# A feed-forward stage that hands products to GpSimd and multiplies by tokens that already carry their norm

## The chip, the cores and the metric

The kernel runs on one core of a Trainium2 chip. The metric is the device time of one execution in microseconds, and shorter is better. Five engines work side by side, each through its own queue, in order: TensorE multiplies matrices (PE in the profile, PEld is its weight load), VectorE does arithmetic on tensors (DVE), ScalarE does activations, casts and copies (ACT), GpSimd does elementwise work on SBUF alone (POOL), and SyncE issues DMAs (SP). An instruction that waits for another engine holds up everything behind it in its own queue.

## The reference

Two layers act on `x`, 512 tokens by 1024 features. Each has a token mixer (differential attention in layer 0, gated linear attention in layer 1) beside a cross-attention into 256 memory tokens, one output projection, and a gated feed-forward stage. The change lies in the feed-forward stage:

```
def conv_ffn(h, w_up, conv_w, conv_b, w_down):
    u = h @ w_up                                   # 1024 -> 2 * 2816
    c = depthwise_causal_conv(u, conv_w) + conv_b  # width 3 over the tokens
    a, g = jnp.split(c, 2, axis=-1)
    return (jax.nn.silu(g) * a) @ w_down           # 2816 -> 1024
...
        h = rms_norm(x, ffn_norm[i])
        x = x + conv_ffn(h, w_up[i], conv_w[i], conv_b[i], w_down[i])
```

`rms_norm` multiplies each token by one number of its own, 1/rms, and each feature by a gain. The number of a token can be applied to `h` ahead of the product or to `u` behind it.

## The kernel before

Features lie on the partitions and the 512 tokens along a row. `x` is eight tiles `xT[k]` of 128 x 512. All products are in fp32r with both operands split in two, a rounded part (`hi`, a cast on ScalarE) and the rest (`lo`, a subtraction on VectorE), and each product takes three matmuls: hi by hi, hi by lo, lo by hi.

Weights come in blocks of 128 x 1024 (`raw`, three buffers, loaded in the order of a plan) and are split into `whi` and `wlo` (six buffers each, `WB`): a cast on ScalarE (L255) and a subtraction on VectorE (L258). A block can be split only when the matmuls that read the buffer's last content are done.

The feed-forward stage, `ffn`, goes through three parts of 4, 4 and 3 up tiles (`HALVES`). An up tile `q` has two column groups `n`, and for each PE runs two products of 24 matmuls: `ua` for the linear half and `ug` for the gated half. The eight tokens' tiles `tokens[k]` are taken one after the other within a product, three matmuls each. They hold `x` times the gain, without 1/rms. That number comes later: `row_scales` computes it for all tokens as the tile `rB` behind the first `ua` and `ug`, and `conv` multiplies each product, in PSUM, by `rB` on VectorE (L1165). Then ScalarE takes the last tap and the bias (L1167), VectorE adds the two other taps (L1168, L1169), ScalarE takes the Silu of the gated half (L1333), and VectorE multiplies the halves (L1334). The result is split (`parts_of`, L1190 on ScalarE and L1191 on VectorE) into `mid` tiles. In most parts four sums and differences of each two such tiles are made too, by `combine`, on GpSimd except for a part's last up tile (L1198 to L1201), since the product with `w_down` uses a scheme of seven products for eight (`seven`); the sums of weight blocks for it are made on GpSimd by `combined` (L287 to L290).

The order of PE's instructions is that of the code. On the other engines a scheduler sets it when the program is built. PSUM has eight banks in four groups of two (`mm`, `sm`, `lg`, `tp`); the up products take them in turn, and the down products by a rule of their own.

Of the kernel before, what the change touches and what calls it, by code (L numbers as in the profile page):

```python
# [11 lines left out]
F32 = mybir.dt.float32  # L12
# [9 lines left out]
S = 512  # L22
# [63 lines left out]
def _pieces():  # L86

    plan = []

    def piece(key, name, i, ks, *ranges):  # L90
        plan.append((key, name, i, ks, ranges))

    for l in range(2):
        if l == 0:
            w = "w_in_diff"
            piece(("qk", 0), w, 0, K8, (0, 256), (768, 1024))
            for key in ORDER:
                if key[0] == "qk":
                    p = key[1]
                    piece(key, w, 0, K8, (256 * p, 256 * p + 256), (768 + 256 * p, 1024 + 256 * p))  # L100
                elif key[0] == "kv":
                    piece(key, "w_mem_kv", key[1], K8, (0, 512))
                elif key[0] == "vm":
                    p = key[1]
                    piece(key, w, 0, K8, (1536 + 256 * p, 1792 + 256 * p), (2304, 2560))
                else:
                    p = key[1]
                    piece(key, w, 0, K8, (1536 + 256 * p, 2048 + 256 * p))
        else:
            w = "w_in_gla"  # L110
            piece(("gm", 1), w, 0, K8, (2304, 2576))
            for c in range(5):
                piece(("g", c), w, 0, K8, (512 * c, min(512 * c + 512, 2304)))
        for i, part in enumerate(PASS[l]):
            for c, ks in part:
                piece(("o", l, i, c), "w_out", l, ks, (256 * c, 256 * c + 256))
        base = 0
        for nq in HALVES:
            for q in range(base, base + nq):
                piece(("ua", l, q), "w_up", l, K8, (256 * q, 256 * q + 256))  # L120
# [18 lines left out]

TURNS = ('mm', 'mm', 'sm', 'sm', 'lg', 'lg', 'tp', 'tp')  # L140
# [42 lines left out]
def trunk(ctx, tc, head_d, x_t, mem_t, wpack, cols_a_d, cols_d, conv_d, gate_d, rel_bias, diff_lambda, consts, onehot, out):  # L183
# [94 lines left out]
    def combined(raw, n):  # L278
# [4 lines left out]
        r, wsum = full(raw), sum_pool[0].tile([128, WTILE], F32, name="wsum", bufs=2)  # L283
        a12, a22, a11, a21 = (r[:, :, i] for i in range(4))
        sv = wsum[:, :512 * pairs].rearrange("p (i j c) -> p i j c", i=4, j=pairs)
        s1, s2, s3, s4 = (sv[:, i] for i in range(4))
        ADD.tensor_add(s1, a21, a22)  # L287
        ADD.tensor_sub(s3, a11, a21)
        ADD.tensor_sub(s2, s1, a11)
        ADD.tensor_sub(s4, a12, s2)  # L290
        A.copy(full(h0)[:, :, :3], r[:, :, :3])
        V.tensor_sub(full(l0)[:, :, :3], r[:, :, :3], full(h0)[:, :, :3].bitcast(F32))
        m = slice(0, 512 * pairs)
        A.copy(h1[:, m], wsum[:, m])
        V.tensor_sub(l1[:, m], wsum[:, m], h1[:, m].bitcast(F32))
        out = []
        for j in range(pairs):
            own = lambda t, i: t[:, 512 * j + 128 * i:512 * j + 128 * i + 128]
            new = lambda t, i: t[:, 128 * (pairs * i + j):128 * (pairs * i + j) + 128]
# [3 lines left out]
        return out  # L303

    def make_block(raws=None):
# [9 lines left out]
        if plan[i][0][0] == "dn":  # L315
            made[i] += combined(raw, n)
# [8 lines left out]
    ADD = G  # L325


    def weights(key, by_block=False):
# [3 lines left out]
        if i + 1 < len(plan) and plan[i + 1][0][0] in ("dn", "dw"):  # L332
            limit = first_of[i + 1] + 1
# [814 lines left out]
    def ffn(pool, l, acc):  # L1148
        rB = pool.tile([128, S], F32, name="rB", bufs=1)
        sum_pool[0] = pool  # L1150
        old = list(zip(xh, xl))
        nu = [0]
# [4 lines left out]
        def up(parts, n, ops):  # L1157
            i = nu[0]
            nu[0] += 1
            p = bank(TURNS[i % 8])  # L1160
            product(p, parts, n, ops)
            return p

        def conv(p, j):
            V.tensor_mul(p, p, rB)  # L1165
# [27 lines left out]
        left, right = blk(0, 256), blk(1, 256)  # L1193

        def combine(b2, b1, bh, bl, fh, fl, E):
            t = pool.tile([128, 2 * S], F32, name="tsum", bufs=1)
# [5 lines left out]
            h, lo = (pool.tile([128, 2 * S], F32R, name="mid2", bufs=9) for _ in range(2))  # L1202
            for c in ((blk(0, S), blk(1, S)) if E is V else (blk(0, 2 * S),)):
                parts_of(t[:, c], h[:, c], lo[:, c])
            two = lambda hi, lw, c: (hi[:, c], lw[:, c])
            return [(fh, fl), two(bh, bl, left), two(bh, bl, right), two(h, lo, q[3]),
                    two(h, lo, q[0]), two(h, lo, q[1]), two(h, lo, q[2])]
# [4 lines left out]
        def down(base, nq, mids, pairs, tags, last, acc2):  # L1212
            first = used[0]
            whole = [plan[first + c][0][0] == "dw" for c in range(4)]
            sizes = [1 if plan[i][0][0] != "dn" else 2 for i, _, _ in order]
            live = sum(sizes[first_of[first]:done[0]])
            banks, seen = {}, [set() for _ in range(4)]

            def refill():
                nonlocal live  # L1220
                while done[0] < min(len(order), first_of[min(used[0] + 2, len(plan))]) and live + sizes[done[0]] <= WB:
                    live += sizes[done[0]]
                    make_block()

            def start(c):
                assert plan[used[0]][0][1:] == (l, base, c)
                used[0] += 1
                if whole[c] and l == 0:
                    banks[c] = [bank("lg"), bank("tp")]
                else:  # L1230
                    ta, tb = (("mm", "sm"), ("lg", "tp"))[(c + tags) % 2]
                    banks[c] = [bank(t) for t in ((ta, tb) if whole[c] else (ta, ta, tb, tb))]
                refill()

            def release(c, m):
                nonlocal live
                piece = first + c
                if m == nq - 1 or m % 2:
                    live -= 1 if whole[c] else 2
                    refill()  # L1240

            def seven(c, m, some=steps):
                for i in some:
# [7 lines left out]
                release(c, m)  # L1251
                if m == nq - 1:
                    made[first + c] = None
# [17 lines left out]
            def eight(c, n, m0, m1, total=nq):  # L1271
                parts = made[first + c]
                product(banks[c][n], parts, n, pairs, range(2 * m0, 2 * m1), 2 * total)

            if all(whole):
                refill()
                for c0 in (0, 2):
                    cs = (c0, c0 + 1)
                    for c in cs:
# [3 lines left out]
                        release(c, 1)  # L1283
                    for c in cs:
# [4 lines left out]
                        release(c, nq - 1)  # L1289
                        made[first + c] = None  # L1290
                return
            refill()
# [8 lines left out]
            if whole[3]:  # L1301
                start(3)
                while done[0] < first_of[first + 4]:
                    make_block()
# [5 lines left out]
                for t, tag, queue in ((left, "mm", nc.sync), (right, "sm", nc.scalar)):  # L1310
                    p = bank(tag)[:, :S // 2]
# [5 lines left out]
        base, tokens, acc2 = 0, old, None  # L1317
        for part, nq in enumerate(HALVES):
            mids, pairs = [], []
            nu[0] = 0  # L1320
            last = part == len(HALVES) - 1
            for q in range(base, base + nq):
                wa = weights(("ua", l, q))
                wg, c2, ops = None, [], []
                for n in range(2):
                    ua = up(wa, n, tokens)
                    wg = wg or weights(("ug", l, q))
                    ug = up(wg, n, tokens)
# [4 lines left out]
                    A.activation(cg, cg, AF.Silu)  # L1333
                    V.tensor_mul(ca, ca, cg)  # L1334
                    c2.append(ca)
                    if n == 0 or last:
                        ops += [mid_tile(), mid_tile()]
                        parts_of(ca, *ops[-2:])
                        pairs.append(ops[-2:])
                    else:  # L1340
                        m = mid_tile()
                        ops += [m[:, left], m[:, right]]
                        parts_of(ca[:, left], *ops[-2:])
                if last:
                    ops[2:] = [t[:, left] for t in ops[2:]]
                if not last or l == 1:
                    mids.append(combine(*c2, *ops, V if q == base + nq - 1 else ADD))
# [7 lines left out]
            down(base, nq, mids, pairs, nu[0] // 4 % 2, last, acc2)  # L1355
# [88 lines left out]
```

## Time and profile before

| | us |
|---|---|
| median of 3 runs | 1149.63 (1149.50 to 1149.68) |
| profiled execution, its own time | 1150.36 |
| its span, first to last instruction | 1148.5 |
| PE busy | 1142.7 (99%) |
| VectorE busy | 871.2 (76%) |
| ScalarE busy | 592.0 (52%) |
| GpSimd busy | 193.2 (17%) |

The profiled execution took 0.73 us more than the median, and 1.86 us of its time lies outside its span. Layer 0's feed-forward stage begins on PE at 240.69 us and its third up tile at 284.67 us; in layer 1 these are 792.43 and 836.40 us. Durations in the rows are of single instructions, and neighbours on an engine overlap by up to 0.1 us. A matmul of 128 x 512 has a modelled end: its length in a row is 0.39 us, but the next one starts 0.22 to 0.23 us after it.

### The profile page before, as it was taken

To read this page: it belongs to the slowest core of one execution; us is meant where nothing else is said; L and a number is where in the kernel's file an instruction comes from. 1 tells how busy PE (TensorE), PEld (TensorE's weight loads), DVE (VectorE), ACT (ScalarE), POOL (GpSimd) and SP (SyncE) were. 2 spreads that over 40 slices of the span, in tenths; PEclk is the share of its full clock that TensorE was granted. 3 is DMA by queue.
4 is the path that set the end of the run, shared out by engine and by line. 5 is a ranking of instruction groups with operands and counts; after the bars stand their busy time and mean duration, and the time that the engine had idled before them with its cause. 6 is when DMAs were issued, how large, how long until landed. Compare 5 with 4: busy or idle time off the path is not lost.

```text
span 1148.5 us, 16655 instructions
## 1 busy us (share of the span) xinstructions
PE 1142.7 (99%) x6311; PEld 985.1 (86%) x6311; DVE 871.2 (76%) x1455; ACT 592.0 (52%) x1032; POOL 193.2 (17%) x230
## 2 busy tenths in 40 slices
PE   9999999999999999999999999999999999999998
PEld 7888888888899888988888888988888988899887
DVE  8576778688789677977677637777887977797777
ACT  6676686555454354434457634535644444453442
POOL 0000000001543125500000000000135403360340
PEclk9999999999999999999999999999999999999999
DMA  9522242133214322343252220333241342234212
GB/s 293 173 83 84 78 142 74 58 109 110 92 57 146 111 77 80 96 144 100 69 182 70 100 94 12 101 125 119 74 126 40 127 149 74 61 91 143 92 46 102
DMA packets 39662, 117.83 MB, mean 103 GB/s; under 512 B 4767, under 2 KB 7256, under 8 KB 39582
## 3 DMA queue, kind: packets, MB, share of 16 engines
q1 hardware_dynamic: 39150, 116.37, 31.8%
q8 instruction: 50, 0.82, 0.3%
q10 hardware_dynamic: 432, 0.39, 0.1%
q14 instruction: 30, 0.25, 0.1%
HBM read 112.54 MB, written 4.21 MB: 102 GB/s over the span
## 4 chain that ended last, share of the span: by engine, by line
PE 99%; DMA 0%; DVE 0%; ACT 0%; issue 0%
PE ps_mm L365 6%; PE ps_mm L367 6%; PE ps_mm L366 6%; PE ps_mm L387 6%; PE ps_mm L388 6%; PE ps_mm L389 6%; PE ps_lg L1247 5%; PE ps_sm L388 5%; PE ps_sm L389 5%; PE ps_sm L387 5%; PE ps_mm L1247 4%; PE ps_tp L388 4%; PE ps_lg L388 4%; PE ps_tp L387 4%; PE ps_lg L387 4%; PE ps_tp L389 4%
## 5 line engine op out<-in xcount | busy, mean ns | idle before, releaser
L258 DVE TENSOR_TENSOR wlo<-raw,whi 128x1024 fp32r<-128x1024 f32 (+4 forms) x174 | 194.2, 1127 | 77.0 <-ACT whi L255 76.4
L255 ACT CAST whi<-raw 128x1024 fp32r<-128x1024 f32 (+4 forms) x174 | 168.0, 976 | 124.2 <-PE ps_sm L388 29.8
L365 PE MATMUL ps_mm<-whi,xsh 128*128 128x512 f32 (+2 forms) x328 | 126.2, 385 | 0.0
L367 PE MATMUL ps_mm<-whi,xsl 128*128 128x512 f32 (+2 forms) x328 | 123.0, 375 | 0.0
L366 PE MATMUL ps_mm<-wlo,xsh 128*128 128x512 f32 (+2 forms) x328 | 122.8, 374 | 0.0
L387 PE MATMUL ps_mm<-xsh,whi 128*128 128x512 f32 x278 | 109.3, 393 | 0.0
L388 PE MATMUL ps_mm<-xsl,whi 128*128 128x512 f32 x278 | 108.4, 390 | 0.0
L389 PE MATMUL ps_mm<-xsh,wlo 128*128 128x512 f32 x278 | 108.2, 389 | 0.0
L387 PE MATMUL ps_sm<-xsh,whi 128*128 128x512 f32 x218 | 84.8, 389 | 0.0
L388 PE MATMUL ps_sm<-xsl,whi 128*128 128x512 f32 x218 | 84.8, 389 | 0.0
L389 PE MATMUL ps_sm<-xsh,wlo 128*128 128x512 f32 x218 | 84.8, 389 | 0.0
L365 PEld LDWEIGHTS ps_mm<-whi,xsh 128*128 128x128 f32 x328 | 61.7, 188 | 11.4 <-issue 1.0
L367 PEld LDWEIGHTS ps_mm<-whi,xsl 128*128 128x128 f32 x328 | 61.7, 188 | 11.3
L366 PEld LDWEIGHTS ps_mm<-wlo,xsh 128*128 128x128 f32 x328 | 61.8, 188 | 10.1
L387 PE MATMUL ps_lg<-xsh,whi 128*128 128x512 f32 x160 | 62.2, 389 | 0.0
L388 PE MATMUL ps_lg<-xsl,whi 128*128 128x512 f32 x160 | 62.2, 389 | 0.0
L389 PE MATMUL ps_lg<-xsh,wlo 128*128 128x512 f32 x160 | 62.2, 389 | 0.0
L387 PE MATMUL ps_tp<-xsh,whi 128*128 128x512 f32 x160 | 62.2, 389 | 0.0
L388 PE MATMUL ps_tp<-xsl,whi 128*128 128x512 f32 x160 | 62.2, 389 | 0.0
L389 PE MATMUL ps_tp<-xsh,wlo 128*128 128x512 f32 x160 | 62.2, 389 | 0.0
L389 PEld LDWEIGHTS ps_mm<-xsh,wlo 128*128 128x128 f32 x278 | 52.2, 188 | 11.0
L387 PEld LDWEIGHTS ps_mm<-xsh,whi 128*128 128x128 f32 x278 | 52.2, 188 | 10.8 <-issue 0.3
(382 smaller groups left out, 2835.4 us busy)
## 6 DMA issues: line engine op xcount, KB each, us to landing
raw<-in_wpack_dram SPq DMA_DIRECT2D x178, 512.0 KB, 3.5
xt<-in_x_t_dram SPq DMA_DIRECT2D x15, 256.0 KB, 5.2
raw<-in_wpack_dram SPq DMA_DIRECT2D x15, 256.0 KB, 3.1
raw<-in_wpack_dram SPq DMA_DIRECT2D x8, 384.0 KB, 3.0
xres<-xt SPq DMA_DIRECT2D x8, 256.0 KB, 3.2
xt<-xres SPq DMA_DIRECT2D x8, 256.0 KB, 5.8
out_dram<-xt SPq DMA_DIRECT2D x7, 256.0 KB, 2.0
bt<-bias_d SPq DMA_DIRECT2D x6, 256.0 KB, 4.1
```

Of the source, the lines that this page charges most:

```text
L255: ins = A.copy(hi[:, c], raw[:, c])
L258: V.tensor_sub(lo[:, c], raw[:, c], hi[:, c].bitcast(F32))
L365: mm(p, sh[k][:, blk(b)], hi, start=k == 0, stop=False)
L366: mm(p, sh[k][:, blk(b)], lo, start=False, stop=False)
L367: mm(p, sl[k][:, blk(b)], hi, start=False, stop=k == KT - 1)
L387: mm(p, hi[:, blk(n)], bh, start=i == first, stop=False)
L388: mm(p, hi[:, blk(n)], bl, start=False, stop=False)
L389: mm(p, lo[:, blk(n)], bh, start=False, stop=i == last)
L1247: mm(banks[c][b][:, h], w, v, start=b not in seen[c], stop=m == nq - 1 and t == 2 and i in close)
```

## The change

From the third up tile of each layer on (`SCALED = 2`) the products use scaled tokens, `fresh`. While the first two up tiles run, each `xT[k]` is multiplied by `rB` on GpSimd (`scaled`), by the gain on ScalarE, and split by `parts_of`: eight products, sixteen ScalarE instructions and eight VectorE subtractions a layer. Three tokens are made behind each of the second and third column groups and two behind the fourth. Up tiles 2 to 10 then need no product with `rB` in `conv`. The gating product is made on GpSimd except in the last up tile of each part. The sums of `combine` and `combined` share two buffers (`wsum`; before, there were two and one), `mid2` has eight buffers for nine, PSUM banks are taken in one rotation by all products, and weight blocks are asked for whenever two (or one) of the six buffers have been used up (`refill`, `release`), in the up products too. `dynamic_dma_scratch_size=512` frees memory for the tokens' tiles `hsc`. `SEVEN` is empty, so that the code for it (`up_by_seven`, `token_sums`, `plain`) makes no instruction. PE has as many instructions as before, of the same shapes.

```
+SCALED = 2
+SEVEN = ()
...
-        def conv(p, j):
-            V.tensor_mul(p, p, rB)
+        def conv(p, j, scaled):
+            if not scaled:
+                V.tensor_mul(p, p, rB)
...
+        def scaled(k):
+            t = ctile()
+            G.tensor_mul(t, xT[k], rB)
+            A.activation(t, t, AF.Copy, scale=c_ffn(l, k))
+            return t
+
+        def scaled_token(k):
+            t = scaled(k)
+            if k < 6:
+                y = pool.tile([128, 2 * S], F32R, name="hsc", bufs=6)
+                hi, lo = y[:, :S], y[:, S:]
+            else:
+                hi, lo = split_tiles()
+            parts_of(t, hi, lo)
+            return hi, lo
...
             for q in range(base, base + nq):
-                wa = weights(("ua", l, q))
+                if q == SCALED:
+                    tokens = fresh
...
-                    ca = conv(ua, 2 * q + n)
-                    cg = conv(ug, 22 + 2 * q + n)
+                    cn = ca[n] if ca else conv(ua, 2 * q + n, q >= SCALED)
+                    cg = conv(ug, 22 + 2 * q + n, q >= SCALED)
                     A.activation(cg, cg, AF.Silu)
-                    V.tensor_mul(ca, ca, cg)
+                    end = q == base + nq - 1
+                    (V if end else G).tensor_mul(cn, cn, cg)
...
+                    if 0 < 2 * q + n < 4:
+                        fresh += [scaled_token(k) for k in range(len(fresh), min(len(fresh) + 3, KT))]
...
+        def take(n):
+            nb[0] += n
+            return [bank(TURNS[i % 8]) for i in range(nb[0] - n, nb[0])]
+
+        def refill():
+            nonlocal live
+            while done[0] < min(len(order), first_of[min(used[0] + 2, len(plan))]) and live + sizes[done[0]] <= WB:
+                live += sizes[done[0]]
+                make_block()
...
+        def up(i, n):
+            p, = take(1)
+            product(p, whole_piece(i), n, tokens)
+            if n == 1:
+                release(i, 2, True)
             return p
```

GpSimd's queue in layer 0, before, from the first sums of up tiles on (`cvo` are results of `conv`, `raw` is a weight block):

```order
L1198 TENSOR_TENSOR tsum_2833<-cvo_2819 128x256
L1200 TENSOR_TENSOR tsum_2833<-cvo_2753,cvo_2819 128x256
L1199 TENSOR_TENSOR tsum_2833<-cvo_2753,tsum_2833 128x256
L1201 TENSOR_TENSOR tsum_2833<-cvo_2753,tsum_2833 128x256
L1198 TENSOR_TENSOR tsum_2997<-cvo_2983 128x256
L1200 TENSOR_TENSOR tsum_2997<-cvo_2917,cvo_2983 128x256
L1199 TENSOR_TENSOR tsum_2997<-cvo_2917,tsum_2997 128x256
L287 TENSOR_TENSOR wsum_3211<-raw_3053 128x256
```

The same queue in the changed kernel, from the fourth token (`xt_1744`) to the sums of the second up tile:

```order
L1294 TENSOR_TENSOR cvo_2950<-xt_1744,rB_2659 128x512
L1294 TENSOR_TENSOR cvo_2956<-xt_1746,rB_2659 128x512
L1294 TENSOR_TENSOR cvo_2962<-xt_1748,rB_2659 128x512
L1428 TENSOR_TENSOR cvo_2935<-cvo_2935,cvo_2940 128x512
L1294 TENSOR_TENSOR cvo_3045<-xt_1750,rB_2659 128x512
L1294 TENSOR_TENSOR cvo_3052<-xt_1752,rB_2659 128x512
L1428 TENSOR_TENSOR cvo_3031<-cvo_3031,cvo_3036 128x512
L1271 TENSOR_TENSOR wsum_3061<-cvo_3031 128x256
```

Eight token products and four gating products of 128 x 512 have come in among the sums; those of the last two tokens stand behind the gating product of the second up tile's first column group (`cvo_2935`).

ScalarE's queue in layer 0, before, from the last weight casts ahead of the end of the second up tile on (its last product is `ps_tp_2957`):

```order
L255 CAST whi_3043<-raw_2889 128x1024 [waits DMAHW1_49,PE_49]
L255 CAST whi_3049<-raw_3010 128x1024 [waits DMAHW2_49,PE_49]
L1167 ACTIVATE cvo_2988<-ps_tp_2957,cv0_81 128x512 [waits DVE_49]
L1333 ACTIVATE cvo_2988<-cvo_2988 128x512 [waits DVE_49,Activation_49]
L1190 CAST mid_2994<-cvo_2983 128x256 [waits DVE_49]
L1190 CAST mid2_3002<-tsum_2997 128x1024 [waits Pool_49]
L1167 ACTIVATE cvo_3081<-ps_mm_3018,cv0_81 128x512 [waits DVE_49]
```

The same place in the changed kernel (that last product is `ps_tp_3005`, `cvo_3045` is the seventh token, `cvo_3052` the eighth):

```order
L1242 ACTIVATE cvo_3036<-ps_tp_3005,cv0_81 128x512 [waits DVE_49]
L1295 ACTIVATE cvo_3045<-cvo_3045,cols_80 128x512 [waits Pool_49]
L1295 ACTIVATE cvo_3052<-cvo_3052,cols_80 128x512 [waits Pool_49]
L258 CAST whi_3074<-raw_2997 128x1024 [waits DMAHW2_49,PE_49]
L1426 ACTIVATE cvo_3036<-cvo_3036 128x512 [waits DVE_49,Activation_49]
L1265 CAST mid_3042<-cvo_3031 128x256 [waits Pool_49]
L1265 CAST xsh_3048<-cvo_3045 128x512 [waits Activation_49]
L1265 CAST xsh_3055<-cvo_3052 128x512 [waits Activation_49]
```

The casts of the last two tokens' `hi` parts now stand behind the Silu of the second up tile's last product and behind a cast that waits for GpSimd's gating of it.

PE's queue at the third up tile of layer 0, in the changed kernel, from the sixth token on (the weights are `whi_2878` and `wlo_2879`):

```order
L398 MATMUL ps_mm_3080<-hsc_2965,whi_2878 128x512 [waits Activation_49]
L399 MATMUL ps_mm_3080<-hsc_2965,whi_2878 128x512 [waits DVE_49]
L400 MATMUL ps_mm_3080<-hsc_2965,wlo_2879 128x512
L398 MATMUL ps_mm_3080<-xsh_3048,whi_2878 128x512 [waits Activation_49]
L399 MATMUL ps_mm_3080<-xsl_3049,whi_2878 128x512 [waits DVE_49]
L400 MATMUL ps_mm_3080<-xsh_3048,wlo_2879 128x512
```

Where the kernel before reads tokens that were ready before the stage began, each token's first two matmuls now wait for a cast and for a subtraction.

More of the change, by code (lines that the diff above doesn't have):

```diff
@@ L303, in combined, with by_seven, sum_tile @@
         return out
+    def by_seven(i):
+        key = plan[i][0]
+        return key[0] == "dn" or key[0] == "ua" and key[2] in SEVEN
+    def sum_tile():
+        return sum_pool[0].tile([128, WTILE], F32, name="wsum", bufs=2)
     def make_block(raws=None):
@@ L314, in make_block @@
             made.append([])
-        if plan[i][0][0] == "dn":
-            made[i] += combined(raw, n)
+        if by_seven(i):
+            made[i] += combined(raw, n, int(plan[i][0][0] == "ua" and not made[i]))
         else:
@@ new lines, in up_by_seven @@
+        def up_by_seven(i):
+            b, seen = take(4), set()
+            where = [(2, left), (0, left), (0, right), (1, left), (3, right), (2, right), (3, left)]
+            for m, ks in enumerate(((6, 7), (4, 5), (0, 1), (2, 3))):
+                while len(made) <= i or len(made[i]) <= m:
+                    refill()
+                part = made[i][m]
+                if m == 0:
+                    for n in range(2):
+                        product(b[n], part, n, [tokens[k] for k in ks], range(2), 99)
+                else:
+                    for r in steps:
+                        c, h = where[r]
+                        (hi, lo), (vh, vl) = part[r], sums_of[ks][r]
+                        for t, (w, v) in enumerate(((hi, vh), (hi, vl), (lo, vh))):
+                            mm(b[c][:, h], w, v, start=c > 1 and c not in seen, stop=m == 3 and t == 2 and r in (2, 5, 6, 3))
+                            seen.add(c)
+                if m % 2:
+                    release(i, 2, m == 3)
+            u, w = ctile(), ctile()
+            A.copy(u[:, left], b[2][:, left])
+            V.tensor_add(w[:, right], u[:, left], b[2][:, right])
+            V.tensor_add(u[:, right], w[:, right], b[3][:, right])
+            V.tensor_add(w[:, left], w[:, right], b[3][:, left])
+            V.tensor_add(w[:, right], u[:, right], b[3][:, left])
+            V.tensor_add(b[0], b[0], u)
+            V.tensor_add(b[1], b[1], w)
+            return b[:2]
@@ L1235, in release, with emitted, seven @@
-            def release(c, m):
-                nonlocal live
-                piece = first + c
+            def start(c):
+                begin(("dw" if whole[c] else "dn", l, base, c))
+                banks[c] = take(2 if whole[c] else 4)
+            def emitted(c, m):
                 if m == nq - 1 or m % 2:
-                    live -= 1 if whole[c] else 2
+                    release(first + c, 1 if whole[c] else 2, m == nq - 1)
+            def seven(c, m, some=steps):
+                while len(made) <= first + c or len(made[first + c]) <= m:
```

166 lines of the change are left out of this document (91 added, 75 removed).

## The prediction

> **What bounds the kernel now.** I read the page first, then PE's waits, then PE's timeline at the start of the third up tile.
>
> ```profile
> span 1148.5 us, 16655 instructions
> PE 1142.7 (99%) x6311; PEld 985.1 (86%) x6311; DVE 871.2 (76%) x1455; ACT 592.0 (52%) x1032; POOL 193.2 (17%) x230
> PE 99%; DMA 0%; DVE 0%; ACT 0%; issue 0%
> PE ps_tp L492 <- PEq L1399: 0.8, 1, 0.8
> PE ps_mm L566 <- DVE whi L528: 0.4, 1, 0.4
> PE ps_mm L566 <- ACT xsh L345: 0.2, 1, 0.2
> ```
>
> The first three lines are the page's, the other three are all of PE's waits that the trace names (total, times, longest): 1.4 us in the whole span, all at its start. A busy PE could still hide stalls, since ends are modelled, so I looked at starts (columns: start, length).
>
> ```profile
> 284.44 0.39 PE L389 MATMUL ps_tp<-xsh,wlo 128*128 128x512 f32 x1
> 284.67 0.39 PE L387 MATMUL ps_mm<-xsh,whi 128*128 128x512 f32 x1
> 284.89 0.39 PE L388 MATMUL ps_mm<-xsl,whi 128*128 128x512 f32 x1
> ...
> 288.75 0.39 PE L387 MATMUL ps_mm<-xsh,whi 128*128 128x512 f32 x1
> ...
> 840.48 0.39 PE L387 MATMUL ps_mm<-xsh,whi 128*128 128x512 f32 x1
> ```
>
> The second row is the first matmul of up tile 2, the fourth the first of its seventh token: 18 matmuls in 4.08 us, 0.227 each. Up tile 2 follows up tile 1 without a gap, and that step is kept through both feed-forward stages. The change leaves PE the same instructions. So PE has nothing to give there: time taken off VectorE is worth nothing, and each microsecond that PE is made to wait is lost.
>
> **The change, part by part.** The costs:
>
> ```profile
> L1165 DVE TENSOR_TENSOR ps_sm<-ps_sm,rB 128x512 f32<-128x512 f32 x9 | 6.2, 694 | 0.4 <-PE ps_sm L389 0.4
> L1334 DVE TENSOR_TENSOR cvo<-cvo 128x512 f32<-128x512 f32 x17 | 13.2, 777 | 6.1 <-ACT cvo L1333 6.1
> L1191 DVE TENSOR_TENSOR mid<-cvo,mid 128x512 fp32r<-128x512 f32 x11 | 7.5, 686 | 0.8 <-ACT mid L1190 0.7
> L258 DVE TENSOR_TENSOR wlo<-raw,whi 128x1024 fp32r<-128x1024 f32 x33 | 39.9, 1219 | 4.8 <-ACT whi L255 4.8
> L1169 DVE SCALAR_TENSOR_TENSOR cvo<-ps_mm,cv,cvo 128x510 f32<-128x510 f32 x9 | 6.7, 748 | 0.3
> L1191 DVE TENSOR_TENSOR mid<-tsum,mid 128x1024 fp32r<-128x1024 f32 x4 | 5.0, 1259 | 13.2 <-ACT mid L1190 13.2
> L1167 ACT ACTIVATE cvo<-ps_sm,cv 128x512 f32<-128x512 f32 x9 | 7.0, 778 | 0.9 <-DVE ps_sm L1165 0.9
> L1333 ACT ACTIVATE cvo<-cvo 128x512 f32<-128x512 f32 x17 | 10.7, 631 | 20.0 <-DVE cvo L1169 20.0
> L345 ACT ACTIVATE xsh<-xt,cols 128x512 fp32r<-128x512 f32 x16 | 11.5, 716 | 3.9 <-DVE xt L1111 3.9
> L1190 ACT CAST mid<-cvo 128x512 fp32r<-128x512 f32 x11 | 6.8, 618 | 3.3 <-DVE cvo L1334 3.1
> L288 POOL TENSOR_TENSOR wsum<-raw 128x128 f32<-128x128 f32 x3 | 1.4, 462 | 0.0
> L1201 POOL TENSOR_TENSOR tsum<-cvo,tsum 128x256 f32<-128x256 f32 x14 | 10.3, 737 | 0.7
> ```
>
> VectorE loses 72 products with rB (0.694) and 32 gating products (0.777) and gains 16 subtractions (0.686): 50.0 + 24.9 - 11.0, some 64 us less. All of it lies beside PE's work: 0. Banks in one rotation, the buffer counts and the requests for weights cost 0: the products take the banks that they took, six split blocks stay in reach, and the cover is the block held ahead (an up product of 24 x 0.227 = 5.4 us); if that fails, a block's cast and subtraction (about 2 us) come to light each time.
>
> What costs is the new wait: PE at up tile 2 needs tokens that are made while up tiles 0 and 1 run. A GpSimd product of 512 columns is in no row. From 462 ns at 128 and 737 at 256 the line gives 737 + 2 x 275, about 1.28 us. So GpSimd gets 8 token products and 3 gating products ahead of the last gating that matters, besides 4 sums: 11 x 1.28 + 4 x 0.74 = 17 us. And it shares something with VectorE:
>
> ```profile
> 346.91 1.18 POOL L288 TENSOR_TENSOR wsum<-raw 128x256 f32<-128x256 f32 x1
> 348.05 1.45 POOL L289 TENSOR_TENSOR wsum<-wsum,raw 128x256 f32<-128x256 f32 x1
> ...
> 347.41 1.49 DVE L292 TENSOR_TENSOR wlo<-raw,whi 128x768 fp32r<-128x768 f32 x1
> 348.82 1.75 DVE L295 TENSOR_TENSOR wlo<-wsum,whi 128x1024 fp32r<-128x1024 f32 x1
> ...
> 482.38 0.74 POOL L290 TENSOR_TENSOR wsum<-raw,wsum 128x256 f32<-128x256 f32 x1
> ...
> 482.40 0.68 DVE L1263 TENSOR_TENSOR xt<-xt,ps_lg 128x512 f32<-128x512 f32 x1
> ```
>
> Where VectorE has two SBUF inputs, the two take turns, one whole instruction each, and both are longer by the wait (0.74 becomes 1.18 to 1.45). Where one input is PSUM (last pair), neither is. A hold of 1.28 us by a 512-wide product is in no row; if the port were given back after 0.74, as the rows show it for 256, some 2 us less would be lost a layer. The Trainium skill, "SBUF — State Buffer", section "Who interferes with whom", calls this an exclusive lock for the whole instruction, so by it the long hold is full. I take 1.28.
>
> Now the queue, in layer 0. Its clock starts with the first Silu, which the change doesn't touch:
>
> ```profile
> 262.53 0.63 ACT L1333 ACTIVATE cvo<-cvo 128x512 f32<-128x512 f32 x1
> ...
> 816.98 0.63 ACT L1333 ACTIVATE cvo<-cvo 128x512 f32<-128x512 f32 x1
> ...
> core 0: us, PE busy (x) PEld busy (x) DVE busy (x) ACT busy (x) POOL busy (x), PEclk, DMA share, GB/s
> 240.69:284.67 43.98, 43.98 (x196) 36.41 (x194) 34.66 (x47) 22.83 (x31) 3.06 (x4) 1.00 0.35 110
> 792.43:836.40 43.97, 43.97 (x196) 36.41 (x194) 34.41 (x46) 25.98 (x34) 3.05 (x4) 1.00 0.29 90
> ```
>
> In these two up tiles VectorE is busy 34.7 of 44 us already. From 263.8 to its product of up tile 1's last bank with rB, its queue in the changed kernel holds 9 tap additions, 4 products with rB, 3 weight subtractions, 8 of 512, one of 1024 and one of 256: by the rows, less 0.08 of overlap each, 18 us. Without waits it gets there at 282, ahead of PE's end of up tile 1 (284.8). But it waits in order. I walked the three queues by hand: for the first gating and the hold behind it 1.9; for the third token's cast 1.4; for the sums' cast, which stands ahead of the first product with rB of up tile 1's gated half, 3.0; for ScalarE's Identity behind that 0.8; then for the holds of gating and of tokens 7 and 8 1.3, 0.7 and 1.3; small ones 0.5. Together 10.9, so it arrives at about 292.3 instead of 284.8.
>
> From there nothing can be hidden, since the seventh token's cast stands on ScalarE behind the gating of that last bank: VectorE 3.8 (product 0.6, tap 0.7, weight subtraction 1.1, taps 1.4), Silu 0.6, GpSimd's gating 1.3 (plus waits 0.4), cast of mid 0.4, cast of token 7 0.6: ready at 299.4. PE wants it at 288.75: 10.6 lost. Then token 7's subtraction alternates with GpSimd's sums (1.2 lost) and so does token 8's (0.6). Token 6 may cost 0.8 before that, within the 10.6. Layer 0: 12.4. In layer 1 the same queue starts 24.6 us behind the stage's start (816.98 - 792.43) and not 21.8 (262.53 - 240.69): 2.7 later, 15.1. Sum 27.5. VectorE and GpSimd catch up while PE waits, and later tiles use tokens that are there.
>
> Bounds: with no waits at all in the queues, the last chain alone remains: 284.8 + 3.8 + 0.6 + 1.3 + 0.4 + 0.6 = 291.5, against 288.75, and the two subtractions 1.2: 4.0 a layer, 8 in sum. Upwards: the row at 348.05 has 1.45 us for 0.74. If each of the 11 long products and 4 sums ahead of the last gating were stretched like that, they would take 11 x 2.5 + 4 x 1.45 = 33.3 us and end at 297.1; in my walk the eighth token's product ends at 288.6. That is 8.5 more a layer, 44 in sum. A gain is excluded, as PE's step shows no slack that could be won. I take 27.5, whose turns are those of the rows.
>
> PE's clock may add to it:
>
> ```profile
> 1143.73 0.28 PE L389 MATMUL ps_sm<-mid,wlo 128*128 128x256 f32 x1
> ...
> 1146.00:1148.50 2.50, 0.00 (x0) 0.00 (x0) 0.00 (x0) 0.00 (x0) 0.00 (x0) 0.73 0.02 3
> ```
>
> Some 2 to 4 us after the last matmul the granted clock falls. How slow matmuls are after such a pause, no row shows; I put it into the upper end. The Trainium skill, "TensorE: Matmul & The Clock Gate", Part 1, gives half rate after about 3.4 us of idling and 3.4 us of work to come back, by which each pause would cost an estimated 1.7 us more and the sum would be 31.
>
> The profiled execution: span 1148.5 + 27.5 = 1176.0, plus 1.86 around it 1177.9; its own time was 0.73 above the median, so the median becomes 1149.6 + 27.5 = 1177.
>
> **The rivals.** (1) The queues keep up, and only the last chain shows: +8, 1157.6; with part of the waits up to 1168. For it: the scheduler put the token products ahead of the last gating on GpSimd, and GpSimd was 17% busy. Against it stand VectorE's waits for such sums in the kernel before, 3.2 and 4.0 us, with less in the queues than now:
>
> ```profile
> 295.68 1.36 DVE L1191 TENSOR_TENSOR mid<-tsum,mid 128x1024 fp32r<-128x1024 f32 x1 [3.20 <-ACT mid L1190]
> ...
> 318.32 1.23 DVE L1191 TENSOR_TENSOR mid<-tsum,mid 128x1024 fp32r<-128x1024 f32 x1 [4.00 <-ACT mid L1190]
> ```
>
> (2) More: each wait lengthens the next, or the clock falls: 1186 to 1194. For it: the row at 348.05 and the fall of the clock. (3) No loss, 1149.6: the tokens are there at 288.75 and 840.48. It decides whether ScalarE can reach the seventh token's cast within 4.0 us of up tile 1's end. Against it: the chain above takes 6.7 without a single wait. A gain would need PE to have had stalls. (4) GpSimd becomes the bound of every up tile: two gatings 2.6 and four sums 3.0, twice that with turns, stay within a tile's 96 x 0.227 = 21.8 us; so only a small part of (2).
>
> **How the numbers follow.** Forecast, 1168 to 1186: 0.62. Rival 1, 1154 to 1168: 0.18. Rival 2, above 1186: 0.14. Rival 3: 0.06, of which 0.02 faster by over 0.2% (2.3 us, about what a measurement of this kernel can tell). Slower 0.94. The range takes in the forecast, most of rival 1 and the nearer part of rival 2: 1156 to 1192.
>
> **What would show it.** In the profile after, PE's first product of up tile 2 has a wait of 8 to 17 us at its seventh token, once a layer, released by ScalarE's cast of it, and no other wait in the stage; the granted clock dips behind it; VectorE's busy time falls by some 60 us and GpSimd's rises by the 32 gating and 16 token products, 48 x 1.28 = 61 us or more; token products on GpSimd last 1.3 to 2.5 us. A wait of 4 us there means rival 1; waits spread over many up tiles, or at weight buffers, would make the prediction wrong in kind, and none at all wrong altogether.

## The result and the profile after

| kernel | median, us | lowest to highest | ratio to before, 95% interval |
|---|---|---|---|
| before (4 runs beside it) | 1149.66 | 1149.50 to 1151.12 | |
| changed (4 runs) | 1180.10 | 1179.16 to 1180.52 | 1.0261 [1.0243, 1.0279] |

The change costs 30.4 us. The profiled execution took 1179.73 us. Its page (the span, the engines' busy times, the chain that ended last by engine), and after it all waits of PE that the trace names (total, times, longest):

```profile
span 1177.9 us, 16669 instructions
PE 1150.2 (98%) x6311; PEld 989.0 (84%) x6311; DVE 827.7 (70%) x1367; ACT 607.3 (52%) x1064; POOL 264.4 (22%) x278
PE 93%; DVE 3%; POOL 2%; ACT 1%; issue 1%; ACTq 0%; POOLq 0%; DVEq 0%
```

```profile
PE ps_mm L398 <- ACT xsh L1265: 21.0, 2, 11.8
PE ps_mm L399 <- DVE hsc L1266: 1.7, 2, 1.0
PE ps_mm L399 <- DVE xsl L1266: 1.0, 2, 0.5
PE ps_tp L503 <- PEq L1497: 0.8, 1, 0.8
```

PE has its 6311 matmuls and a new wait, twice, for the `hi` part of a token. The timeline of the changed kernel shows which, in layer 0 and in layer 1 (start, length, idle time before):

```profile
288.32 0.39 PE L398 MATMUL ps_mm<-hsc,whi 128*128 128x512 f32 x1
289.74 0.50 PE L399 MATMUL ps_mm<-hsc,whi 128*128 128x512 f32 x1 [1.04 <-DVE hsc L1266]
290.08 0.39 PE L400 MATMUL ps_mm<-hsc,wlo 128*128 128x512 f32 x1
299.71 0.79 PE L398 MATMUL ps_mm<-xsh,whi 128*128 128x512 f32 x1 [9.24 <-ACT xsh L1265]
300.98 0.80 PE L399 MATMUL ps_mm<-xsl,whi 128*128 128x512 f32 x1 [0.48 <-DVE xsl L1266]
301.58 0.63 PE L400 MATMUL ps_mm<-xsh,wlo 128*128 128x512 f32 x1
302.00 0.63 PE L398 MATMUL ps_mm<-xsh,whi 128*128 128x512 f32 x1
...
868.03 0.80 PE L398 MATMUL ps_mm<-xsh,whi 128*128 128x512 f32 x1 [11.80 <-ACT xsh L1265]
```

It is the seventh token of up tile 2, at 299.71, released by ScalarE's cast. Behind the wait the matmuls follow each other by 0.43 us instead of 0.227 until 306.4. The windows view gives the granted clock for it (third column from the end):

```profile
288.00:290.30 2.30, 1.26 (x6) 0.54 (x4) 2.30 (x2) 2.30 (x3) 1.14 (x1) 1.00 0.00 0
290.30:293.70 3.40, 0.17 (x1) 0.00 (x0) 3.40 (x5) 0.57 (x2) 0.00 (x0) 0.85 0.58 146
293.70:297.00 3.30, 0.00 (x0) 0.00 (x0) 3.26 (x5) 2.95 (x5) 0.00 (x0) 0.50 0.71 215
...
303.00:306.40 3.40, 3.40 (x10) 2.63 (x9) 2.60 (x3) 1.41 (x2) 0.00 (x0) 0.51 0.00 0
306.40:310.00 3.60, 3.60 (x18) 2.97 (x17) 0.04 (x1) 0.00 (x0) 0.00 (x0) 1.00 0.02 5
```

I add up what the start-to-start times have over 0.224 us (0.120 for 256 columns), stage by stage; below this sum is called PE's loss. It is 14.4 us at up tile 2 of layer 0, 15.8 at that of layer 1, 0.3 at the last `w_down` products and nothing elsewhere in the feed-forward stages: 30.5. The span grew by 29.4, as the part of it behind PE's last matmul became 1.2 us shorter.

The timeline of the side engines up to that cast, in the changed kernel, and after it three of its groups by line, GpSimd's new products and the subtractions of tokens (busy time, mean ns of one):

```profile
292.54 0.68 DVE L1240 TENSOR_TENSOR ps_tp<-ps_tp,rB 128x512 f32<-128x512 f32 x1
...
296.54 0.63 ACT L1426 ACTIVATE cvo<-cvo 128x512 f32<-128x512 f32 x1 [0.35 <-DVE cvo L1244]
...
297.25 1.45 POOL L1428 TENSOR_TENSOR cvo<-cvo 128x512 f32<-128x512 f32 x1 [8.11 <-ACT cvo L1426]
...
299.04 1.14 ACT L1265 CAST xsh<-cvo 128x512 fp32r<-128x512 f32 x2
```

```profile
L1428 POOL TENSOR_TENSOR cvo<-cvo 128x512 f32<-128x512 f32 x32 | 43.7, 1365 | 360.7 <-ACT cvo L1426 360.7
...
L1294 POOL TENSOR_TENSOR cvo<-xt,rB 128x512 f32<-128x512 f32 x16 | 25.3, 1605 | 0.1
...
L1266 DVE TENSOR_TENSOR hsc<-cvo,hsc 128x512 fp32r<-128x512 f32 x12 | 11.9, 1007 | 2.8 <-ACT hsc L1265 2.8
```

VectorE reaches up tile 1's last bank at 292.54, Silu, gating and the casts follow, and the seventh token's `hi` part is ready at 299.7. So far all is as forecast. Is the wait then the whole cost?

### The profile page after: what moved, and what is told of

Read it like the earlier page. It is cut to its first block, busy times and chain, and to the rows that moved or that the text cites. A ratio compares the mean times of both kernels' runs of the same rounds, so it can differ in the third digit from the quotient of the medians.

```text
span 1177.9 us, 16669 instructions
## 1 busy us (share of the span) xinstructions
PE 1150.2 (98%) x6311; PEld 989.0 (84%) x6311; DVE 827.7 (70%) x1367; ACT 607.3 (52%) x1064; POOL 264.4 (22%) x278
## 4 chain that ended last, share of the span: by engine, by line
PE 93%; DVE 3%; POOL 2%; ACT 1%; issue 1%; ACTq 0%; POOLq 0%; DVEq 0%
PE ps_mm L376 6%; PE ps_mm L378 6%; PE ps_mm L399 6%; PE ps_mm L377 6%; PE ps_mm L400 6%; PE ps_mm L398 6%; PE ps_lg L1342 5%; PE ps_sm L398 5%; PE ps_sm L399 5%; PE ps_sm L400 5%; PE ps_mm L1342 4%; PE ps_tp L1342 3%; PE ps_sm L1342 3%; PE ps_tp L398 3%; PE ps_lg L398 3%; PE ps_tp L400 3%
## 5 line engine op out<-in xcount | busy, mean ns | idle before, releaser
L261 DVE TENSOR_TENSOR wlo<-raw,whi 128x1024 fp32r<-128x1024 f32 (+4 forms) x174 | 199.6, 1159 | 106.4 <-ACT whi L258 105.2
L258 ACT CAST whi<-raw 128x1024 fp32r<-128x1024 f32 (+4 forms) x174 | 167.9, 976 | 119.3 <-PE ps_sm L399 27.9
L1428 POOL TENSOR_TENSOR cvo<-cvo 128x512 f32<-128x512 f32 x32 | 43.7, 1365 | 360.7 <-ACT cvo L1426 360.7
L398 PE MATMUL ps_mm<-xsh,whi 128*128 128x512 f32 x158 | 63.8, 404 | 21.0 <-ACT xsh L1265 21.0
L378 PEld LDWEIGHTS ps_mm<-whi,xsl 128*128 128x128 f32 x328 | 61.7, 188 | 11.3
L301 ACT CAST whi<-wsum 128x1024 fp32r<-128x1024 f32 (+1 forms) x38 | 38.6, 1017 | 51.1 <-POOL wsum L293 50.3
L399 PE MATMUL ps_mm<-xsl,whi 128*128 128x512 f32 x158 | 62.9, 398 | 1.0 <-DVE xsl L1266 1.0
L302 DVE TENSOR_TENSOR wlo<-wsum,whi 128x1024 fp32r<-128x1024 f32 (+1 forms) x38 | 47.3, 1244 | 22.1 <-ACT whi L301 22.0
L400 PE MATMUL ps_mm<-xsh,wlo 128*128 128x512 f32 x158 | 62.5, 396 | 0.0
L1266 DVE TENSOR_TENSOR mid<-cvo,mid 128x512 fp32r<-128x512 f32 (+1 forms) x44 | 31.1, 707 | 40.0 <-ACT mid L1265 40.0
L1342 PE MATMUL ps_lg<-mid,whi 128*128 128x256 f32 x304 | 58.6, 283 | 0.0
L1342 PE MATMUL ps_mm<-mid,whi 128*128 128x256 f32 x280 | 54.0, 283 | 0.0
L399 PE MATMUL ps_mm<-hsc,whi 128*128 128x512 f32 x120 | 47.7, 398 | 1.7 <-DVE hsc L1266 1.7
L290 POOL TENSOR_TENSOR wsum<-raw 128x256 f32<-128x256 f32 (+1 forms) x38 | 37.3, 980 | 54.2 <-DVE wlo L302 49.4
```

Of the source, the lines that this page charges most:

```text
L258: ins = A.copy(hi[:, c], raw[:, c])
L261: V.tensor_sub(lo[:, c], raw[:, c], hi[:, c].bitcast(F32))
L378: mm(p, sl[k][:, blk(b)], hi, start=False, stop=k == KT - 1)
L398: mm(p, hi[:, blk(n)], bh, start=i == first, stop=False)
L399: mm(p, hi[:, blk(n)], bl, start=False, stop=False)
L400: mm(p, lo[:, blk(n)], bh, start=False, stop=i == last)
```

## The experiments

Each is an edit of the changed kernel. "G" is gating on GpSimd as in the change, "V" on VectorE; "shared" are the two `wsum` buffers that the sums of weights and of token products take in turn, "own" a `tsum` buffer for the latter.

| run | tokens from | gating | sums | median, us | ratio, 95% interval |
|---|---|---|---|---|---|
| changed | tile 2 | G | shared | 1180.10 | 1.0261 [1.0243, 1.0279] |
| e1 | never | G | shared | 1178.17 | 1.0247 [1.0232, 1.0263] |
| e3 | tile 3 | G | shared | 1168.93 | 1.0169 [1.0154, 1.0184] |
| e2 | tile 2 | V | shared | 1172.16 | 1.0196 [1.0181, 1.0211] |
| e6 | tile 2, made 4 + 4 | G | shared | 1165.42 | 1.0140 [1.0123, 1.0157] |
| e8 | never | V | shared | 1156.16 | 1.0061 [1.0043, 1.0079] |
| e12 | never | G | own | 1167.50 | 1.0155 [1.0139, 1.0171] |
| e13 | never | V | own | 1149.31 | 0.9999 [0.9990, 1.0009] |
| e16 | never | V, and a duplicate on G | own | 1168.25 | 1.0157 [1.0142, 1.0173] |
| e15 | tile 3 | V | own | 1151.76 | 1.0015 [1.0005, 1.0024] |
| e18 | tile 2, made 4 + 4 | V | own | 1156.39 | 1.0061 [1.0046, 1.0076] |
| e7 | tile 2, PE kept busy | G | shared | 1178.70 | 1.0252 [1.0236, 1.0269] |

**Without tokens (e1).**

```
-SCALED = 2
+SCALED = 99
...
-                    if 0 < 2 * q + n < 4:
-                        fresh += [scaled_token(k) for k in range(len(fresh), min(len(fresh) + 3, KT))]
```

> No scaled tokens are made or used: every up product is multiplied by rB on VectorE as before, and all else of the change (gating on GpSimd, banks in one rotation, requests for weights by free buffers) stays. Theory A, the loss is only the wait for late tokens at up tile 2: 1149.7 us within 0.6, no wait of PE in the feed-forward stages, VectorE busy some 850 us, GpSimd some 240. Rival B, gating on GpSimd and its holds on VectorE cost by themselves: 1155 to 1165, with waits spread over the stage. Rival C, banks and requests for weights cost: 1152 or more, with PE released by weights or banks.

Measured 1178.17: theory A falls as the whole story. No token is waited for, and PE's loss, 28.7 us, is at other places, as the four largest of this run's waits of PE say:

```profile
PE ps_sm L1342 <- DVE mid L1266: 9.2, 8, 1.3
PE ps_lg L1342 <- DVE wlo L302: 4.9, 5, 1.1
PE ps_mm L1342 <- DVE wlo L302: 2.6, 3, 1.1
PE ps_mm L1342 <- DVE wlo L299: 1.0, 1, 1.0
```

L1342 are the `w_down` products by seven, L302 the split of their weight sums, L1266 that of `mid`. The loss is 4.7 to 6.9 us at each of the five such stages. So the rest of the change has a cost of its own, which the changed kernel doesn't show. But this run gives VectorE the 72 products with `rB` back, so its 28.7 us aren't what lies hidden in the changed kernel. The next run tells how much does.

**Tokens one tile later (e3): `SCALED = 3`.**

> The tokens are made as in the change but first used one up tile later, by up tile 3. Theory A: they are ready 11 us (layer 0) and 9 us (layer 1) before PE then wants the seventh, so both waits and the slow matmuls behind them go: 1149.7 us within 0.6, VectorE busy 3 us more than in the change. Rival B, the queues behind GpSimd's long products stay behind, so that the next tile waits too: 1155 or more. A gain below 1149.1 is expected by neither.

Measured 1168.93; rival B. The token waits are gone (0.3 and 1.4 us of loss in the up tiles), but 7.8 and 9.5 us come up at the first `w_down` products of each layer. Some 17 us, then, lie under the token wait of the changed kernel (e3 has eight products with `rB` more): while PE waits there, the side engines catch up. At the later ones nothing is lost, which isn't so in e1: up tiles 4 to 10 need no product with `rB`, which gives VectorE the time.

**Gating on VectorE (e2), and four tokens at once (e6).**

```
-                    (V if end else G).tensor_mul(cn, cn, cg)
+                    V.tensor_mul(cn, cn, cg)
```

> Gating is back on VectorE in all up tiles; tokens are made on GpSimd and used from up tile 2 as in the change. Theory A with its walk: holds of the first gating (1.9) and of the fourth (1.3) go, the last gating takes 0.76 instead of 1.45 and needs no turn (1.4), three gatings of 0.76 come to VectorE (2.3): 2.3 us less wait a layer, about 7 and 9.5, slow matmuls behind them stay: 1175 us, 1172 to 1178. Rival B, GpSimd's gating is what makes the tokens late: 1150 to 1160.

Measured 1172.16, at the lower end of theory A's range: the loss at up tile 2 is 10.7 and 11.9 us.

```
-                    if 0 < 2 * q + n < 4:
-                        fresh += [scaled_token(k) for k in range(len(fresh), min(len(fresh) + 3, KT))]
+                    if 0 < 2 * q + n < 3:
+                        fresh += [scaled_token(k) for k in range(len(fresh), min(len(fresh) + 4, KT))]
```

> Four tokens are made behind each of the second and third column groups, none behind the fourth, so that the seventh token's cast stands on ScalarE ahead of up tile 1's last Silu and gating. Theory A, the place in ScalarE's queue is what makes the token late: it is ready at about 289 to 291 instead of 299.7 in layer 0, 0 to 3 us of wait a layer, no slow matmuls: 1150 to 1156 us. Rival B, the amount of work on GpSimd and VectorE makes it late wherever it stands: 1170 or more.

Measured 1165.42, between the two: a miss for both. About half the loss goes with the place of the last two tokens in the queues; 6.7 and 8.4 us of it stay, though they stand ahead now.

**Which part costs at the `w_down` products (e8, e12, e13).** On top of e1, e8 has gating on VectorE, e12 the buffer for the sums, e13 both:

```
-            t = sum_tile()
+            t = pool.tile([128, 2 * S], F32, name="tsum", bufs=1)
```

> No scaled tokens, and gating back on VectorE; banks in one rotation, requests by free buffers and the two buffers that the sums of weights and of token products share stay. In the run without tokens PE lost 28.7 us, all of it at the products with w_down. There the weight sums of the first w_down block stand on GpSimd behind the sums of the third up tile (from 319.9 us on, 306.1 before), as both kinds take the two wsum buffers in turn. Theory D, the shared buffers and GpSimd's gating make them late together: gating on VectorE brings the sums 3 to 4 us earlier, and 1 to 3 us stay at each of the five places: 1153 to 1162 us. Rival E, GpSimd's gating alone: 1149.7 within 0.8. Rival F, the order alone: 1170 or more.

> No scaled tokens, gating on GpSimd as in the change, but the sums of token products have a buffer of their own again (tsum, one), so that the sums of the first w_down blocks stand on GpSimd ahead of the gating and the sums of the third up tile. Theory D: the weight blocks are there in time, 1149.7 to 1153 us, PE's waits at the w_down products gone or under 3 us in sum. Rival E, GpSimd's gating alone: 1170 or more, as without the buffer of their own.

> No scaled tokens, gating on VectorE, the sums of token products with a buffer of their own: of the change only the banks in one rotation, the requests by free buffers and eight buffers of mid2 stay. If these cost nothing: 1149.6 us within 0.8, no wait at the w_down products. If they carry a part of the 6.6 us that were lost with shared sums: 1152 or more, with waits for weight blocks.

All these runs multiply every product by `rB`. Under this condition shared sums alone cost 6.6 us (e8, as theory D said), and gating on GpSimd alone costs 18 us (e12: neither D's 1153 nor E's 1170, nearer to E). Without both the kernel is as fast as before (e13). So the banks in one rotation, the requests by free buffers and the eight `mid2` buffers cost nothing, within 0.1%. How shared sums make weights late shows on GpSimd, where the sums of the first `w_down` block begin, in e13, e8 and e1 in this order:

```profile
306.28 1.44 POOL L290 TENSOR_TENSOR wsum<-raw 128x256 f32<-128x256 f32 x1 [8.59 <-DMA raw<-in_wpack_dram]
```

```profile
311.23 0.73 POOL L1271 TENSOR_TENSOR wsum<-cvo 128x256 f32<-128x256 f32 x1 [17.55 <-DVE cvo L1428]
...
313.50 0.73 POOL L290 TENSOR_TENSOR wsum<-raw 128x256 f32<-128x256 f32 x1
```

```profile
316.31 1.29 POOL L1428 TENSOR_TENSOR cvo<-cvo 128x512 f32<-128x512 f32 x1 [9.22 <-ACT cvo L1426]
317.67 0.74 POOL L1271 TENSOR_TENSOR wsum<-cvo 128x256 f32<-128x256 f32 x1
...
319.95 0.73 POOL L290 TENSOR_TENSOR wsum<-raw 128x256 f32<-128x256 f32 x1
```

With a buffer of their own the token sums let the weight sums go ahead as soon as the block has landed (306.28). With shared buffers the weight sums stand behind the third up tile's sums (L1271), which wait for its gating: 7.2 us later with gating on VectorE, 13.7 later with it on GpSimd.

**Why gating on GpSimd costs (e16).** Either GpSimd's time and its turns with VectorE, or the longer way of a result through four queues. e16 keeps gating on VectorE, as e13, and adds a product that nobody reads:

```
+                    if not end:
+                        G.tensor_mul(pool.tile([128, S], F32, name="dup", bufs=1), cg, rB)
```

> As the run with gating on VectorE and a buffer of their own for the sums, and beside each of its 32 gating products GpSimd makes a product of 128 x 512 of the Silu's result and rB into a tile that nobody reads, at the places of its queue where the change has the gating. Theory L (GpSimd's time and the turns that it takes with VectorE make the weight sums and VectorE late): 1160 or more, near the 1167.5 of the run with gating on GpSimd. Theory R (the way VectorE, ScalarE, GpSimd, ScalarE, VectorE that a gating on GpSimd puts into queues that run in order makes VectorE wait): within 2 us of the run without the added products, 1149.5 to 1152.

Measured 1168.25, the time that theory L gave: a GpSimd product that nothing waits for costs as much as the gating itself. The gating of up tile 1's first half on VectorE, in e13 and then in e16, with the duplicate beside it:

```profile
280.61 0.69 DVE L1428 TENSOR_TENSOR cvo<-cvo 128x512 f32<-128x512 f32 x1
...
330.64 0.69 DVE L1240 TENSOR_TENSOR ps_tp<-ps_tp,rB 128x512 f32<-128x512 f32 x1
```

```profile
281.57 1.49 POOL L1430 TENSOR_TENSOR dup<-cvo,rB 128x512 f32<-128x512 f32 x1 [6.14 <-ACT cvo L1426]
...
281.82 1.79 DVE L1428 TENSOR_TENSOR cvo<-cvo 128x512 f32<-128x512 f32 x1
...
335.50 0.68 DVE L1240 TENSOR_TENSOR ps_tp<-ps_tp,rB 128x512 f32<-128x512 f32 x1
```

VectorE's instruction starts 0.25 us into the duplicate, waits it out and ends 0.55 us after it: 1.79 us instead of 0.69. This agrees with the lock for a whole instruction that the Trainium skill names ("SBUF — State Buffer", section "Who interferes with whom"). VectorE's 44 gating products take 48.5 us in e16 and 33.3 in e13. By the last bank of up tile 3 (the rows at 330.64 and 335.50) VectorE is 4.9 us late; in e12 it gets there at 336.24, as late.

But it is late there in another way. VectorE's waits for ScalarE's casts of results, in e13, e16 and e12, and in the last line what holds such casts up in e12 (total, times, longest):

```profile
DVE mid L1266 <- ACT mid L1265: 51.0, 27, 4.0
...
DVE mid L1266 <- ACT mid L1265: 62.2, 27, 4.6
...
DVE mid L1266 <- ACT mid L1265: 111.6, 48, 3.5
...
ACT mid L1265 <- POOL cvo L1428: 52.4, 32, 2.1
```

From 240 us to that last bank VectorE is idle for 21.3 us in e13, 23.2 in e16 and 29.6 in e12, and busy for 69.3, 72.2 and 66.6. In e16 it is late mostly because its instructions last longer, in e12 because it waits for casts that stand behind the gating on GpSimd. That is the way of theory R. So e16 shows that GpSimd's load and the turns are enough to cost 19 us, and not that they are what costs in e12, whose trace speaks for the way through the queues. No run has that way without GpSimd's load, so the shares stay open.

**PE kept busy during the wait (e7).** PE's first product of up tile 2 takes its own bank and the next product's, and in between:

```
+                product(p, parts, n, tokens, range(6), 8)
+                w, v = parts[0][0], tokens[0][0]
+                for t in range(40):
+                    mm(warm, w[:, blk(n)], v, start=t == 0, stop=t == 39)
+                product(p, parts, n, tokens, range(6, 8), 8)
```

> The changed kernel with 40 more matmuls of 128 x 512 (9.1 us) on PE behind the sixth token of up tile 2's first product, into the next product's bank, which that product then starts anew. They fill the wait of 9.4 us in layer 0 and most of that of 12.0 us in layer 1; no token comes earlier. If the matmuls of 427 ns behind the waits come from the pause, they return to 227: 2.4 and 2.0 us less, 1175.7 us, 1175 to 1176.5, granted clock without a dip. If they come from the supply of tokens: 1180.1, or more where the added matmuls outlast the wait.

Measured 1178.70: right in layer 0, wrong in layer 1. The timeline behind the added matmuls (L1210), and after it the granted clock in two windows:

```profile
299.77 0.50 PE L398 MATMUL ps_mm<-xsh,whi 128*128 128x512 f32 x1 [0.17 <-ACT xsh L1272]
...
302.52 0.39 PE L400 MATMUL ps_mm<-xsh,wlo 128*128 128x512 f32 x1
302.75 0.40 PE L398 MATMUL ps_mm<-hsc,whi 128*128 128x512 f32 x1
...
866.16 0.79 PE L398 MATMUL ps_mm<-xsh,whi 128*128 128x512 f32 x1 [2.75 <-ACT xsh L1272]
...
868.02 0.63 PE L400 MATMUL ps_mm<-xsh,wlo 128*128 128x512 f32 x1
868.45 0.63 PE L398 MATMUL ps_mm<-xsh,whi 128*128 128x512 f32 x1
```

```profile
299.50:306.00 6.50, 5.37 (x22) 3.83 (x22) 4.76 (x6) 2.46 (x4) 3.15 (x4) 1.00 0.15 60
...
866.00:873.00 7.00, 6.36 (x14) 4.68 (x15) 5.14 (x6) 2.36 (x4) 3.02 (x3) 0.51 0.01 2
```

In layer 0 the step stays 0.23 and the clock 1.00; with the 9.1 us of the added matmuls PE's loss is 12.4 there, 2.0 less. In layer 1 a wait of 2.75 us was left, the clock halved all the same and stayed so until 872.9, as in the changed kernel, though the token came 1.9 us earlier (866.16, not 868.03): 0.9 us of the gain was lost again.

**All causes mended (e15, e18).** e15 is e3, e18 is e6, both with gating on VectorE and the buffer for the sums; five `cvo` tiles make room for it.

> Tokens made as in the change and used from up tile 3 on, gating on VectorE, a buffer of their own for the sums of token products (five result tiles instead of six for it). If the three causes found (tokens one tile too early, gating on GpSimd, shared sums) are all there is: 1149.6 us within 1.0 and no wait of PE in the feed-forward stages; VectorE about 45 us less busy than before, and no gain by it. If token products on GpSimd keep the weight sums behind: 1153 or more, at the first w_down products of each layer.

Measured 1151.76: 1.2 us over the range, with a loss of 1.8 us at the first `w_down` products of layer 1. VectorE was 851.2 us busy, 20 less than before and not 45: the expectation had left out the 16 subtractions that split the tokens there, 13 us; the other 12 us are not accounted for. What it saves is worth nothing, as PE has nothing to catch up.

> As the change (tokens from up tile 2 on), but four tokens behind each of the second and third column groups, gating on VectorE and a buffer of their own for the sums. With four tokens early and gating on GpSimd the wait was 6.7 and 8.4 us; a GpSimd gating that is gone took 3.7 and 3.9 us off the waits where the tokens stood late. If that holds here: 3 to 4.5 us a layer, 1156 to 1159 us. If the tokens are then there in time: 1149.6 to 1152. Nothing faster than before is expected.

Measured 1156.39, in the first theory's range. Tokens for up tile 2 remain late even so, by 4.1 and 4.7 us of loss in the profiled execution, which took 1158.84.

**Fewer matmuls (c6).** The one way to less than PE's time: e15 with `SEVEN = (5, 6, 7, 8, 9, 10)` and the token sums made two column groups later. Its output isn't the reference's, so only its time is read.

> A candidate: tokens used from up tile 3 on, gating on VectorE, a buffer of their own for the sums of token products (five result tiles instead of six, a smaller scratch for it), and the linear half of up tiles 5 to 10 by seven products for eight. PE then has 12 matmuls of 512 and 63 of 256 instead of 48 of 512 in each of twelve products: 12 x 0.227 + 63 x 0.120 = 10.3 against 10.9 us, 0.6 less each, 7.3 in sum. Theory D (with tokens in time and weight sums in time nothing waits): 1142.4 us within 1.0. Rival: the added sums of weights on GpSimd and of products on VectorE are late, and waits of 5 us or more take the gain: 1147 or more.

Measured 1195.99 (ratio 1.0401 [1.0383, 1.0419]); the rival, and worse. VectorE was busy 930.6 us, GpSimd 348.1, and PE lost 5.9 to 11.3 us at each of the five `w_down` stages. No run here beats the kernel before.

## Why the prediction was right, and where it wasn't

- **The place and the chain.** Right: a wait at the seventh token, once a layer, released by ScalarE's cast. The walk had VectorE at the last bank at 292.3 (measured 292.54) and the cast at 299.4 (299.7). Its own terms, 282 and 10.9, add up to 292.9, which is a slip of 0.6. Of the 10.9 us of waits and turns the trace has 4.4 as idle time of VectorE (263.8 to 292.54) and 5 to 6 as longer instructions, such as a weight subtraction of 2.30 us for 1.21 beside a token product (268.2).
- **The size.** Layer 0: 12.4 us forecast, and a loss of 14.4 of which 2.0 is the clock (e7), so 12.4. Layer 1: 15.1 forecast, and 15.8 of which at most some 1.5 is the clock (seven steps of 0.43 for 0.227, one between), so about 14.3. Without the clock the loss was 27.5 in the forecast and is 26.7.
- **The clock.** It was left out of the sum and put into the upper end, for want of a row. It costs 2.0 and at most about 1.5 us. By the Trainium skill ("TensorE: Matmul & The Clock Gate", Part 1) it would have been an estimated 1.7 each, which agrees in sum with this trace. The half clock itself lasts longer behind the wait than its 3.4 us of work, from the matmul at 299.71 to 306.4, with another wait at its start (the row at 300.98).
- **Busy times.** VectorE lost 43.5 us, not 60: its 12 subtractions of `hsc` took 1.007 us, not 0.686, and the weight subtractions (L261, L258 before) rose from 194.2 to 199.6 us; these two make some 9 of the 16 us. GpSimd rose by 71.2, of which 69.0 are the new products, 1.37 and 1.6 us each where 1.28 was taken as the least. These totals did not enter the sum.
- **The step that failed: "Banks in one rotation, the buffer counts and the requests for weights cost 0".** Banks and requests do (e13), but the shared `wsum` buffers cost 6.6 us where every product is multiplied by `rB` (e8). And rival 4 held GpSimd's load in a tile's 21.8 us to be harmless; under the same condition it costs 18 us (e12), as VectorE falls behind, by 5.6 us at the last bank of up tile 3, and PE then waits at the `w_down` products. With scaled tokens only the first such products of each layer are late, by some 17 us in sum (e3), and 1.8 us of that stay with both causes mended (e15). Both stayed out of sight because PE's wait came first and covered them. So the sum came out right without them, which is luck: the reasons given for the 0 were others. For tokens in time rival 3 gave 1149.6; with the tokens used one up tile later the chip gave 1168.9 (e3).

## What to carry to other kernels

A wait hides what would be late behind it: before a stall is given a price as the gain of mending it, ask what the other engines caught up on meanwhile. Work moved from VectorE to an idle GpSimd isn't free for VectorE when both read SBUF; 32 products that nobody used cost this kernel 19 us (e16 against e13). Nor is it free where the result comes back through queues that run in order: in e12 VectorE's waits for casts rose from 51.0 to 111.6 us. And two uses of one rotating buffer are an order between them: sums that were ready stood 7 to 14 us behind others that were not.

## What was not expected of the hardware

The clock halves on much less than a long pause. In e18 the seventh and eighth tokens' `lo` parts came late, and PE waited 1.6 and 0.3 us. The windows of that run before, with and behind these waits (granted clock third from the end):

```profile
286.00:290.00 4.00, 3.95 (x18) 2.93 (x16) 4.00 (x6) 4.00 (x6) 0.00 (x0) 1.00 0.45 131
290.00:293.30 3.30, 1.48 (x5) 0.95 (x6) 3.30 (x5) 1.57 (x2) 0.00 (x0) 1.00 0.82 221
293.60:296.70 3.10, 3.10 (x9) 2.33 (x8) 3.06 (x5) 1.48 (x3) 0.00 (x0) 0.50 0.35 118
296.70:300.00 3.30, 3.30 (x16) 2.71 (x15) 2.38 (x4) 1.00 (x2) 1.83 (x3) 0.97 0.35 124
```

In the window with the waits, in which PE was still busy for 1.48 of 3.3 us, the clock is full; it is halved for the 3 us behind it, in which PE is busy throughout. The Trainium skill ("TensorE: Matmul & The Clock Gate", Part 1) has it fall after about 3.4 us of idling; here less was enough, as with the 2.75 us of e7. Nor is it the longest wait alone that counts. In e12 the trace names no wait of PE from 890 to 906 us that is longer than 1.1 us, but several add up: between 898.9 and 902.3 the matmuls' starts lie 2.05 us further apart in sum than their usual steps, and from 902.35 to 905.7 the granted clock is 0.50, with PE busy throughout. In e1 the stretch of this length with the longest gaps (343.8 to 347.2) has 1.98 us of them, and the clock stays at 1.00. So in these traces the limit lies near 2 us of gaps in 3.4; more closely it was not tried.
